# How many gate/up pairs of a feed-forward are multiplied directly before the seven-product form takes over

## The chip, the cores and the metric

The kernel runs on one core of a Trainium2 chip. The metric is the device time of one execution in microseconds (us). PE is TensorE, which multiplies matrices; DVE is VectorE, ACT is ScalarE, POOL is GpSimd, and SP is SyncE, which issues most of the transfers.

## The reference

The program computes a four-stage, two-layer streaming encoder on 512 tokens of 1024 features, in float32. Each layer is

```
x += 0.5 * SwiGLU_1(norm(x))
x += Mixer(norm(x))            # layer 0: two attentions; layer 1: gated conv and band attention
x += CrossAttn(norm(x), norm(mem))
x += 0.5 * SwiGLU_2(norm(x))
```

and a SwiGLU (a feed-forward) is

```
g, u = split_cols(h @ w_in, (D_FF, D_FF))      # w_in: 1024 x 5632, D_FF = 2816
return (silu(g) * u) @ w_out                   # w_out: 2816 x 1024
```

There are four feed-forwards: layer 0 first and second, layer 1 first and second. They are called FF1 to FF4 here, in the order in which they run.

## The kernel before, in words

**Precision.** Every float32 operand is split into a high and a low part of type float32r, and a product is three matmuls (`mm3`, high by high, high by low, low by high). ACT makes the high part, DVE the low part (a subtraction). This holds for the weights too: each weight chunk arrives in a tile `raw`, is split into two tiles `w`, and PE reads those. Six `w` tiles and three `raw` tiles circulate.

**A feed-forward in blocks.** The 2816 hidden columns are 22 blocks of 128. A gate/up pair is one block of the gate and the same block of the up projection. The blocks are worked in three parts (`PARTS`: 7, 7 and 8 pairs); behind each part comes its share of the output projection (`out_proj`, tiles `ps_o`), which adds into `x`.

**Two ways to multiply a pair.** The direct way (`proj_t`) needs 8 steps of 3 matmuls for the gate and as many for the up projection, 48 matmuls with 512 columns each. It reads `xh` and `xl`, the split of x times the gain, and the norm's factor (`rrow`) is multiplied in afterwards by DVE (`gate`, `up`: tiles `gs`, `us`). The block way (`Pair`) treats gate and up, the two halves of the 1024 features and the two halves of the tokens as a 2x2 block product and needs seven products instead of eight: 7 products of 4 steps of 3 matmuls with 256 columns, 84 matmuls. It needs sums of weight blocks, which `Sums` makes with an accumulating transfer from POOL's queue and two additions on POOL (tiles `s`), and sums of the normalized activations.

**The block operands.** `Norm.seven` makes these activation sums once per feed-forward: in four rounds (kk = 0 to 3) DVE makes seven half-token tiles (`hn`), ACT writes their high parts and DVE their low parts (tiles `bop`). It can start when `rrow` is there. It needs one slot for `hn` and seven for `bop`, out of nine slots (`tok_slot`); the `hn` slot is given back at its end.

**What runs first.** The first `FILL = 3` pairs of a feed-forward are multiplied the direct way, the other 19 in blocks. In FF1 alone the first pair's gate and up are multiplied together, feature by feature as x arrives (`pair_t`).

**What sets the order.** The order of all engines' instructions is written out ahead of time by a planner (`Sched`): each task is a generator that says what it needs, `price` charges every instruction to a clock of its engine, and at each step the task of the best priority whose needs are met by PE's planned clock goes next. Weight splits have priority 2, `seven` 3, the constants' set-up (`setup`) 4, the main line of matmuls 5; the gate and up tasks and the evacuations have 0 or 1. A price is nothing but a number for the order; on the chip each engine runs its list in that order and waits for semaphores.

**Where a pair's result goes.** The product silu(gate) times up is split and kept until the output projection. In the first part the pairs up to the last direct one but one lie in slots (tiles `gated`, two pairs to a slot); the last direct pair and those behind it reuse the memory of `xh`/`xl` (tiles `gh`, `gl`), which is free when the last direct matmul has read it.

Of the kernel before, what the change touches and what calls it, by code (L numbers as in the profile page):

```python
# [22 lines left out]
S = 512  # L23
# [5 lines left out]

FILL = 3  # L30
HS = S // 2
# [94 lines left out]
class Sched:  # L126
# [39 lines left out]
    def price(self, eng, method, outs, ins):  # L166
# [6 lines left out]
        if eng == "pe":  # L173
            if method == "transpose":
                cost = 0.108
            elif ins[0].dtype == F32R:
                cost = (n + 32) / 2400.0 if n >= 256 else 0.213
            else:
                cost = 0.06
# [88 lines left out]
def tile_trunk(ctx: ExitStack, tc: tile.TileContext, a: dict, out: bass.AP, nsteps: int = 8):  # L268
# [521 lines left out]

    def ffn_plan(w_in, w_oa, w_ob):
        for pi, (j0, j1) in enumerate(PARTS):
            last = None
            for j in range(j0, j1):
                if j < FILL:
                    plan_t(w_in[j])
                    plan_t(w_in[NF + j])
                    continue
# [12 lines left out]
    class Pair:  # L811
# [101 lines left out]
        def end(self):  # L913
# [14 lines left out]
            yield Need([g])  # L928
            gh, gl = self.res()
            yield from split(gh, gl, g)  # L930
            tok_gs.give()
            self.res.ev.set()

    class Gated:


        def __init__(self, tiles, j, where):
            self.tiles, self.j, self.where = tiles, j, where
            self.ev = Event()
            tiles[j] = (None, None, self.ev)  # L940

        def __call__(self):
            if isinstance(self.where, int):
                hi, lo = (cp.tile([P, S], F32R, tag=f"x{c}{self.where}", name=f"g{c}{self.where}")
                          for c in "hl")
            else:
                hi, lo = self.where[:, 0, :], self.where[:, 1, :]
            self.tiles[self.j] = (hi, lo, self.ev)
            return hi, lo

    def ffn(nrm, done):
# [12 lines left out]
        def up(pair, ps, res):  # L964
# [11 lines left out]
            yield Need([gs])  # L976
            gh, gl = res()
            yield from split(gh, gl, gs)
            tok_gs.give()
            res.ev.set()  # L980

        sch.add(nrm.seven(), 3)
        for pi, (j0, j1) in enumerate(PARTS):
            gated, ns, last = {}, 0, None
            for j in range(j0, j1):


                if pi == 0 and j >= FILL - 1:
                    where = j - FILL + 1
                elif pi == 1:  # L990
# [3 lines left out]
                else:  # L994
                    i = j - j0 - 4 * (pi == 2)
                    if i % 2 == 0:
                        yield tok_slot
                        ns += 1
                        sl = slot([2, 2, S], "gated")
                    where = sl[:, i % 2]  # L1000
                res = Gated(gated, j, where)
                if j < FILL:
                    r, pair = [], [Event()]
# [878 lines left out]
    for kind, layer in steps:  # L1882
# [7 lines left out]
        else:  # L1890
            ffn_plan(a[f"{kind}_in{layer}"], a[f"{kind}_oa{layer}"], a[f"{kind}_ob{layer}"])

# [129 lines left out]
```

## Time and profile before

| | us |
|---|---|
| median of three runs | 2306.8 (2306.78 to 2311.2) |
| the profiled execution | 2306.97 |
| its span, first to last instruction | 2305.2 |
| PE busy | 2224.7 (97%) |
| DVE busy | 1462.9 (63%) |
| ACT busy | 1086.7 (47%) |
| POOL busy | 569.1 (25%) |
| granted TensorE clock, mean | 0.987 |

The page of the profile has the busy time of each engine, the span in 40 slices, the transfer queues, the chain of work that ended last, the costliest groups of instructions with the idle time ahead of them, and the transfers. A group is a line, engine, operation and tile names; since all operations go through one helper, almost every row says L106, and the tile names tell the rows apart. Matmuls are pipelined, so that a matmul's own duration (some 290 to 390 ns) is longer than its share of a dense stream; a stream's length divided by its count gives the pace. FF1 runs from 6.7 to about 381 us of the span, FF2 from about 842, FF3 from about 1200 and FF4 from about 1948 us.

### The profile page before, as it was taken

To read this page: it belongs to the slowest core of one execution; us is meant where nothing else is said; L and a number is where in the kernel's file an instruction comes from. 1 tells how busy PE (TensorE), PEld (TensorE's weight loads), DVE (VectorE), ACT (ScalarE), POOL (GpSimd) and SP (SyncE) were. 2 spreads that over 40 slices of the span, in tenths; PEclk is the share of its full clock that TensorE was granted. 3 is DMA by queue.
4 is the path that set the end of the run, shared out by engine and by line. 5 is a ranking of instruction groups with operands and counts; after the bars stand their busy time and mean duration, and the time that the engine had idled before them with its cause. 6 is when DMAs were issued, how large, how long until landed. Compare 5 with 4: busy or idle time off the path is not lost.

```text
span 2305.2 us, 35767 instructions
## 1 busy us (share of the span) xinstructions
PE 2224.7 (97%) x14060; PEld 1993.9 (86%) x14060; DVE 1462.9 (63%) x2327; ACT 1086.7 (47%) x1869; POOL 569.1 (25%) x516
## 2 busy tenths in 40 slices
PE   7899999899999998999998999999999999899999
PEld 5889998889878888899987898989888888789897
DVE  8656575466666677465757564755675667847473
ACT  5535354455554444353544353545543554435352
POOL 2432322432311022222322131414112101213140
PEclk9899999999999999999999999999999999999999
DMA  5465652112232343555544464623123233346472
GB/s 174 113 185 144 176 148 87 65 56 85 90 101 82 101 119 96 151 148 154 163 123 110 126 171 136 182 98 115 53 81 127 93 110 107 111 131 165 136 187 83
DMA packets 108889, 281.56 MB, mean 122 GB/s; under 512 B 11896, under 2 KB 13944, under 8 KB 108720
## 3 DMA queue, kind: packets, MB, share of 16 engines
q1 hardware_dynamic: 84608, 233.94, 30.9%
q0 software_dynamic: 24112, 45.34, 11.0%
q8 instruction: 110, 1.80, 0.3%
q14 instruction: 59, 0.48, 0.1%
HBM read 277.11 MB, written 4.21 MB: 122 GB/s over the span
## 4 chain that ended last, share of the span: by engine, by line
PE 77%; DVE 9%; issue 4%; POOL 4%; DMA 3%; ACT 3%; SPq 0%; POOLq 0%; ACTq 0%; DVEq 0%
PE ps_m L106 46%; PE ps_o L106 24%; DMA s<-ffn_in 2%; DVE w L106 2%; DVE bop L106 2%; POOL qrr L106 1%; PE ps_pv L106 1%; DVE hn L106 1%; POOL qe L106 1%; ACT w L106 1%; PE ps_s L106 1%; DVE xl L106 1%; PE ps_x L106 1%; PE xo L106 1%; PE ps_pt L106 1%
## 5 line engine op out<-in xcount | busy, mean ns | idle before, releaser
L106 PE MATMUL ps_m<-bop,w 128*128 128x256 f32 x6384 | 787.0, 286 | 48.1 <-ACT bop L106 27.5
L106 PEld LDWEIGHTS ps_m<-bop,w 128*128 128x128 f32 x6384 | 781.7, 194 | 54.8 <-ACT bop L106 28.6
L106 ACT ACTIVATE w<-raw 128x1024 fp32r<-128x1024 f32 (+2 forms) x327 | 335.0, 1028 | 426.5 <-PE ps_o L106 240.2
L106 DVE TENSOR_TENSOR w<-raw,w 128x1024 fp32r<-128x1024 f32 (+2 forms) x327 | 396.1, 1211 | 153.9 <-ACT w L106 145.3
L106 POOL TENSOR_TENSOR s<-s,raw 128x512 f32<-128x512 f32 x152 | 231.2, 1521 | 438.8 <-DMA s<-ffn_in 270.0
L106 PE MATMUL ps_o<-gh,w 128*128 128x512 f32 x1024 | 328.1, 389 | 0.0
L106 PE MATMUL ps_m<-xh,w 128*128 128x512 f32 (+1 forms) x848 | 278.4, 396 | 1.2 <-ACT w L106 1.2
L106 DVE TENSOR_TENSOR w<-s,w 128x512 fp32r<-128x512 f32 (+1 forms) x228 | 219.1, 961 | 71.4 <-ACT w L106 47.4
L106 ACT ACTIVATE w<-s 128x512 fp32r<-128x512 f32 (+1 forms) x228 | 174.2, 768 | 121.6 <-POOL s L106 41.7
L106 PEld LDWEIGHTS ps_o<-gh,w 128*128 128x128 f32 x1024 | 192.3, 188 | 39.5
L106 DVE SCALAR_TENSOR_TENSOR x<-ps_o,x 128x512 f32<-128x512 f32 x160 | 108.5, 687 | 182.4 <-PE ps_o L106 182.0
L106 PE MATMUL ps_m<-w,xh 128*128 128x256 f32 x1152 | 218.9, 289 | 0.0
L106 PE MATMUL ps_o<-gl,w 128*128 128x512 f32 x512 | 199.4, 389 | 0.0
L106 PEld LDWEIGHTS ps_m<-xh,w 128*128 128x128 f32 (+1 forms) x848 | 158.1, 187 | 37.6 <-ACT w L106 2.1
L106 POOL DMA_DIRECT2D s<-ffn_in x76 | 92.0, 1210 | 373.8 <-DMA s<-ffn_in 285.2
L106 PEld LDWEIGHTS ps_m<-w,xh 128*128 128x128 f32 x1152 | 179.2, 191 | 2.0 <-issue 1.2
L106 PE MATMUL ps_m<-xl,w 128*128 128x512 f32 (+1 forms) x424 | 166.0, 392 | 0.0
L106 PE MATMUL ps_m<-w,xl 128*128 128x256 f32 x576 | 162.7, 282 | 0.0
L106 PE MATMUL ps_o<-gated,w 128*128 128x512 f32 x576 | 141.2, 389 | 0.0
L106 POOL TENSOR_TENSOR acc<-acc,sq 128x512 f32<-128x512 f32 x42 | 68.7, 1637 | 254.3 <-ACT sq L106 253.4
L106 PEld LDWEIGHTS ps_o<-gated,w 128*128 128x128 f32 x576 | 107.6, 188 | 22.0
L106 PEld LDWEIGHTS ps_o<-gl,w 128*128 128x128 f32 x512 | 96.2, 188 | 19.4
(468 smaller groups left out, 2826.9 us busy)
## 6 DMA issues: line engine op xcount, KB each, us to landing
raw<-ffn_in SPq DMA_DIRECT2D x98, 512.0 KB, 4.8
s<-ffn_in SPq DMA_DIRECT2D x76, 512.0 KB, 4.3
s<-ffn_in POOLq DMA_DIRECT2D x76, 512.0 KB, 5.9
raw<-ffn_oa SPq DMA_DIRECT2D x64, 448.0 KB, 3.4
a<-ffn_in SPq DMA_DIRECT2D x76, 256.0 KB, 3.8
raw<-ffn_ob SPq DMA_DIRECT2D x32, 512.0 KB, 3.5
raw<-x_kv SPq DMA_DIRECT2D x32, 512.0 KB, 3.5
raw<-even_w SPq DMA_DIRECT2D x24, 512.0 KB, 3.4
```

What stands on the lines that cost most here:

```text
L106: r = fn(*args, **kw)
```

## The change

The number of direct pairs becomes five in FF1 and four in the others. The planner's price of a float32r matmul loses its constant: columns over 2400, not columns plus 32. And since five or four direct pairs leave three or four results for slots, which are two slots beside the eight of `seven`, the slot of a result is now taken when the result is split (`Gated.take` waits for it, `Half` shares it between two pairs), and no longer by the main line ahead of the products.

```
-FILL = 3
+FILL = {True: 5, False: 4}
...
-                cost = (n + 32) / 2400.0 if n >= 256 else 0.213
+                cost = n / 2400.0 if n >= 256 else 0.213
...
-    def ffn_plan(w_in, w_oa, w_ob):
+    def ffn_plan(w_in, w_oa, w_ob, fill):
...
-                if j < FILL:
+                if j < fill:
...
-            gh, gl = self.res()
+            gh, gl = yield from self.res.take()
...
+    class Half:
+        def __init__(self):
+            self.ev = Event()
...
-        def __call__(self):
+        def take(self):
...
-                hi, lo = self.where[:, 0, :], self.where[:, 1, :]
+                if self.first:
+                    yield tok_slot
+                    self.where.slot = slot([2, 2, S], "gated")
+                    self.where.ev.set()
+                yield self.where.ev
+                i = 1 - self.first
+                hi, lo = self.where.slot[:, 0, i, :], self.where.slot[:, 1, i, :]
...
-            gh, gl = res()
+            gh, gl = yield from res.take()
...
+        fill = FILL[nrm.first]
...
-                if pi == 0 and j >= FILL - 1:
-                    where = j - FILL + 1
+                if pi == 0 and j >= fill - 1:
+                    where = j - fill + 1
...
-                    if i % 2 == 0:
-                        yield tok_slot
+                    first = i % 2 == 0
+                    if first:
                         ns += 1
-                        sl = slot([2, 2, S], "gated")
-                    where = sl[:, i % 2]
-                res = Gated(gated, j, where)
-                if j < FILL:
+                        half = Half()
+                    where = half
+                res = Gated(gated, j, where, first)
+                if j < fill:
...
+                     FILL[(kind, layer) == steps[0]])
```

Three places of the written-out order show what moves. The first is DVE's list in FF2, around the last round of the block operands (`hn`, then `bop`). Before:

```order
L106 SCALAR_TENSOR_TENSOR hn<-hn 128x256 x2
L106 TENSOR_TENSOR gated<-gs,gated 128x512
L106 TENSOR_TENSOR w<-s_8729,w 128x1024
L106 TENSOR_TENSOR us<-ps_m,rrow 128x512
L106 TENSOR_TENSOR gs<-gs,us 128x512
L106 TENSOR_TENSOR bop<-hn,bop 128x3x256
L106 TENSOR_TENSOR bop<-hn,bop 128x4x256
L106 TENSOR_TENSOR gl_9028<-gs,gh_9027 128x512
L106 TENSOR_TENSOR g<-ps_m,u 128x256
```

With the change:

```order
L107 SCALAR_TENSOR_TENSOR hn<-hn 128x256 x2
L107 TENSOR_TENSOR gated<-gs,gated 128x512
L107 TENSOR_TENSOR w<-raw,w 128x1024
L107 TENSOR_TENSOR us<-ps_m,rrow 128x512
L107 TENSOR_TENSOR gs<-gs,us 128x512
L107 TENSOR_TENSOR w<-raw,w 128x1024
L107 TENSOR_TENSOR bop<-hn,bop 128x3x256
L107 TENSOR_TENSOR bop<-hn,bop 128x4x256
L107 TENSOR_TENSOR gated<-gs,gated 128x512
L107 TENSOR_TENSOR gs<-ps_m,rrow 128x512
L107 TENSOR_TENSOR w<-s_8824,w 128x512
L107 TENSOR_TENSOR us<-ps_m,rrow 128x512
```

The split of a weight sum (`w<-s`) that stood ahead of the last `bop` rows has gone behind them, with another one that stood further up; in their place stand the split of the fourth pair's up weights and that of the first block pair's first chunk (both `w<-raw`). The third pair's `gated` split and the fourth pair's gate stand behind the last `bop` rows.

The second is ACT's list in FF1, where the constants are set up. Before, this stands between two evacuations (`u`) of the second block pair of the first part:

```order
L106 ACTIVATE v__629<-ps_m 128x256
L106 ACTIVATE e_gcol<-e_gcol 128x1
L106 ACTIVATE o_gcol<-o_gcol 128x1
L106 ACTIVATE e_gcol<-e_gcol 128x1
L106 ACTIVATE setup<-setup 128x64
L106 ACTIVATE subln<-subln 128x1
L106 ACT_TABLE_LOAD
L106 ACTIVATE lsm<-lsm 128x2
```

With the change it stands in the second part, behind that part's first products:

```order
L107 ACTIVATE w<-s_1022 128x1024
L107 ACTIVATE w<-raw 128x1024
L107 ACTIVATE e_gcol<-e_gcol 128x1
L107 ACTIVATE o_gcol<-o_gcol 128x1
L107 ACTIVATE e_gcol<-e_gcol 128x1
L107 ACTIVATE setup<-setup 128x64
L107 ACTIVATE subln<-subln 128x1
L107 ACT_TABLE_LOAD
```

The same work has moved whole from the first part of FF1 into its second part.

The third is PE's list in the mixer of layer 0, around its first transposes of a query tile (`qt`), which wait for POOL's scaling of `qe`. Before:

```order
L106 MATMUL ps_m<-w,xl_3719 128x256
L106 MATMUL ps_m<-w,xh_3626 128x256 x2
L106 MATMUL ps_m<-w,xl_3627 128x256
L106 MATMUL ps_m<-w,xh_3637 128x256 x2
L106 MATMUL ps_m<-w,xl_3638 128x256
L106 MATMUL qt<-ident,qe 128x128 x4
L106 MATMUL ps_m<-w,xh_3679 128x256 x2
```

With the change:

```order
L107 MATMUL ps_m<-w,xh_3597 128x256 x2
L107 MATMUL ps_m<-w,xl_3598 128x256
L107 MATMUL ps_m<-w,xh_3505 128x256 x2
L107 MATMUL ps_m<-w,xl_3506 128x256
L107 MATMUL qt<-ident,qe 128x128 x4
L107 MATMUL ps_m<-w,xh_3516 128x256 x2
```

The buffers have other numbers. Counted from the mixer's first projection matmul, 126 of them stood ahead of these transposes before, and 135 stand there now; of the next three groups of `qt` transposes the counts go from 156, 222 and 252 to 168, 225 and 258.

More of the change, by code (lines that the diff above doesn't have):

```diff
@@ L932, in end, with __init__ @@
             self.res.ev.set()
+    class Half:
+        def __init__(self):
+            self.ev = Event()
     class Gated:
-        def __init__(self, tiles, j, where):
-            self.tiles, self.j, self.where = tiles, j, where
+        def __init__(self, tiles, j, where, first=False):
+            self.tiles, self.j, self.where, self.first = tiles, j, where, first
             self.ev = Event()
             tiles[j] = (None, None, self.ev)
-        def __call__(self):
+        def take(self):
             if isinstance(self.where, int):
@@ L985, in ffn @@
             for j in range(j0, j1):
-                if pi == 0 and j >= FILL - 1:
-                    where = j - FILL + 1
+                first = False
+                if pi == 0 and j >= fill - 1:
+                    where = j - fill + 1
                 elif pi == 1:
@@ L1890, in tile_trunk @@
         else:
-            ffn_plan(a[f"{kind}_in{layer}"], a[f"{kind}_oa{layer}"], a[f"{kind}_ob{layer}"])
+            ffn_plan(a[f"{kind}_in{layer}"], a[f"{kind}_oa{layer}"], a[f"{kind}_ob{layer}"],
+                     FILL[(kind, layer) == steps[0]])
     def store(d):
```

## The prediction, made before the changed kernel was run

> **What bounds the kernel now.** I read the page's engine table first, then the costliest groups with their idle time, then PE by stretches, then PE's timeline where it is idle. The engine table and two groups:
>
> ```profile
> span 2305.2 us, 35767 instructions
> PE 2224.7 (97%) x14060; PEld 1993.9 (86%) x14060; DVE 1462.9 (63%) x2327; ACT 1086.7 (47%) x1869; POOL 569.1 (25%) x516
> ...
> L106 PE MATMUL ps_m<-bop,w 128*128 128x256 f32 x6384 | 787.0, 286 | 48.1 <-ACT bop L106 27.5
> ...
> L106 PE MATMUL ps_o<-gh,w 128*128 128x512 f32 x1024 | 328.1, 389 | 0.0
> ```
>
> PE is busy 97% of the span and idle 80.5 us. Of that idle time 48.1 us stand ahead of the block matmuls, and most of it waits for `bop`, the block operands that DVE and ACT make at the start of each feed-forward. PE by stretches (columns: stretch, length, busy time of PE, PEld, DVE, ACT, POOL, then granted clock, DMA share, GB/s) shows where:
>
> ```profile
> 43.00:86.00 43.00, 25.40 (x159) 23.89 (x158) 31.70 (x62) 20.38 (x38) 18.23 (x37) 0.72 0.36 103
> 381.00:640.00 259.00, 246.21 (x1858) 218.40 (x1856) 160.70 (x323) 140.49 (x294) 92.06 (x110) 1.00 0.23 75
> 640.00:682.00 42.00, 37.90 (x187) 30.25 (x186) 27.66 (x56) 23.38 (x51) 2.07 (x6) 0.96 0.31 101
> 871.30:905.00 33.70, 24.33 (x181) 23.80 (x181) 24.96 (x35) 15.63 (x25) 8.71 (x6) 0.85 0.46 130
> 905.00:1193.00 288.00, 288.00 (x1939) 267.60 (x1939) 171.40 (x244) 129.35 (x206) 71.33 (x51) 1.00 0.51 142
> 1552.00:1720.00 168.00, 163.54 (x1107) 143.77 (x1106) 105.58 (x222) 83.43 (x168) 44.50 (x54) 1.00 0.26 83
> ```
>
> Away from its start a feed-forward has no gap at all (288.00 of 288.00): there only the number and pace of the matmuls count. At its start PE stands still and the granted clock falls to 0.72 and 0.85. The two mixers leave 12.8 + 4.1 us and 4.5 us idle.
>
> **The pace of the two forms.** Two unbroken pieces of the chain of waits (start, length, what) give it:
>
> ```profile
> 1070.75 77.75 PE ps_m L106 x648
> 1034.68 36.07 PE ps_o L106 x159
> ```
>
> A block matmul of 256 columns takes 77.75 / 648 = 0.120 us, one of 512 columns 36.07 / 159 = 0.227 us. So a block pair is 84 x 0.120 = 10.08 us of PE and a direct pair 48 x 0.227 = 10.89 us: each swap costs 0.81 us, and the change makes five (two in FF1, one in each other), 4.0 us. The old price (columns plus 32) met this pace; the new one is below it.
>
> The Trainium skill, "TensorE: Matmul & The Clock Gate", section "Back-to-back issue gap", has columns/2.4 plus 2.5 ns, which is 109 and 216 ns; by that rule a swap would be an estimated 10.36 - 9.17 = 1.19 us and the five 5.9 us. It speaks against the change more than the trace does; the two rows above differ from it, and they decide.
>
> **The stall that the swaps cover, FF2 to FF4.** PE's timeline around FF2's first block products, and where the output projection begins in FF2, FF3 and FF4 with the first block matmul of FF3 and FF4 (a bracket is the idle time before and its releaser):
>
> ```profile
> 871.34 1.23 PE L106 MATMUL ps_m<-bop,w 128*128 128x256 f32 x9
> 878.55 0.58 PE L106 MATMUL ps_m<-bop,w 128*128 128x256 f32 x1 [5.98 <-ACT bop L106]
> 882.52 38.55 PE L106 MATMUL ps_m<-bop,w 128*128 128x256 f32 x302 [3.39 <-DVE bop L106]
> ...
> 921.07 2.06 PE ps_o L106 x9
> ...
> 1229.24 1.23 PE L106 MATMUL ps_m<-bop,w 128*128 128x256 f32 x9
> ...
> 1279.36 2.07 PE ps_o L106 x9
> ...
> 1977.34 1.23 PE L106 MATMUL ps_m<-bop,w 128*128 128x256 f32 x9
> ...
> 2027.03 2.07 PE ps_o L106 x9
> ```
>
> From the first block matmul to the output projection pass 49.73, 50.12 and 49.69 us, 149.5 together. In each lie four block pairs less the 24 matmuls that stand behind the projection's first nine: 312 x 0.120 = 37.4 us. So each loses some 12.3 us, of which 5.98 + 3.39 = 9.4 are idle and the rest slower matmuls at the lowered clock. The same skill page, section "What's actually happening", halves the clock after an idle window of about 3.4 us; the low clock behind the 5.98 us wait agrees. If the waits that remain are shorter, the clock should hold.
>
> With the change, 48 direct and 228 block matmuls stand there: 10.89 + 27.36 = 38.25 us, 114.8 for the three. That is 34.8 us less, minus what waits remain. For those I walk along DVE in FF2, which is the engine that is late:
>
> ```profile
> 846.30 0.69 DVE L106 TENSOR_TENSOR gs<-ps_m,rrow 128x512 f32<-128x512 f32 x1 [0.35 <-ACT rrow L106]
> ...
> 862.36 2.15 DVE L106 TENSOR_TENSOR bop<-hn,bop 128x256 fp32r<-128x256 f32 x3
> ...
> 868.86 1.22 DVE L106 TENSOR_TENSOR w<-raw,w 128x1024 fp32r<-128x1024 f32 x1
> 870.00 0.68 DVE L106 TENSOR_TENSOR gs<-ps_m,rrow 128x512 f32<-128x512 f32 x1
> 870.60 0.68 DVE L106 TENSOR_TENSOR w<-s,w 128x512 fp32r<-128x512 f32 x1
> 871.20 4.30 DVE L106 TENSOR_TENSOR bop<-hn,bop 128x512 fp32r<-128x512 f32 x3
> ...
> 877.66 0.88 DVE L106 SCALAR_TENSOR_TENSOR hn<-hn 128x256 f32<-128x256 f32 x2
> ...
> 881.52 2.08 DVE L106 TENSOR_TENSOR bop<-hn,bop 128x768 fp32r<-128x768 f32 x2
> ...
> 871.43 3.79 POOL L106 TENSOR_TENSOR s<-s,raw 128x512 f32<-128x512 f32 x2 [11.83 <-DVE w L106]
> ```
>
> DVE works nearly without a gap from 846.3 to 883.6. In the changed list the same stretch, up to the last `bop`, has one 1024-column split more (1.22), one 512-column split less (0.68) and the same eleven gate and up steps: the operands are ready at about 884.1. Where POOL adds at the same time a `bop` round takes 4.30 instead of 2.15 us; the additions stand later in the changed program, since their loads come behind the fourth pair's, but may still hit the last rounds, so I leave that cost in. PE now comes there at 871.34 + 10.89 = 882.2, and needs the last round nine matmuls later, at 883.3: 0.8 us of wait in place of 9.4.
>
> Two things are late next. The fourth pair's up weights are split only behind the third round's batch and the fourth `hn` batch, at 878.5 (the end of the `hn` row above) less 0.7 for the sum's split that has gone, plus 0.6 for a `gated` split and 1.1 of its own, so 879.5 with POOL's additions in the way (two rounds, 2.15 each) and 875.2 without; PE wants them half a pair after 871.34, at 876.8: between 0 and 2.7 us. And behind the last `bop` DVE's list has a `gated` split, a gate, two steps of the up projection and two weight splits (0.6 each, the last 1.2 us, some 5 together), while the third product wants the last of them 36 matmuls (4.3 us) after the first: about 1 us. What waits on DVE's queue behind these is only the next pair's evacuation, which has a bank of its own. I take 3 us per feed-forward (bounds 0.5 and 6): 34.8 - 9 = **25.8 us** saved (17 to 33).
>
> **FF1.** Its first block matmuls and the start of its output projection:
>
> ```profile
> 43.02 0.63 PE L106 MATMUL ps_m<-bop,w 128*128 128x256 f32 x4
> ...
> 50.49 0.58 PE L106 MATMUL ps_m<-bop,w 128*128 128x256 f32 x1 [6.17 <-ACT bop L106]
> ...
> 76.08 28.95 PE L106 MATMUL ps_m<-bop,w 128*128 128x256 f32 x216 [3.23 <-ACT u L106]
> 104.87 1.55 PE L106 MATMUL ps_o<-gated,w 128*128 128x512 f32 x6
> ...
> 59.39 2.18 DVE L106 TENSOR_TENSOR bop<-hn,bop 128x768 fp32r<-128x768 f32 x2
> ```
>
> Here 61.85 us pass for the same 37.4 us of matmuls. With two pairs more ahead it is 96 x 0.227 + 144 x 0.120 = 39.1 us, 22.8 less, minus what remains. The operands came at 61.6 in the old program (last row); two more direct pairs put the block products at 43.0 + 21.8 = 64.8, and DVE's list up to the last `bop` has three 1024-column splits of chunks and two gate steps more (3.7 + 1.3) and the splits of one sum of 512 and one of 1024 columns less (0.7 + 1.2), about 3 us more: again just in time. What does not vanish is the set-up of the constants, the 3.23 us wait for `u` behind it on ACT. It moves from a stretch that was stalled anyway into the second part, where PE had no other wait; I charge it in full, with a little lower clock, 4 us, and 2 us for late weights and the first evacuation. That is 6 (bounds 2 and 12), so **16.8 us** saved (11 to 21).
>
> **The price.** A cheaper matmul makes the planner put more matmuls between a task and what it waits for. In the steady feed-forward this changes nothing, PE has no gap there. In the mixers it does; the PE waits of layer 0's mixer and its end (waited for: total, times, longest):
>
> ```profile
> PE qt L106 <- POOL qe L106: 8.6, 11, 1.4
> PE kt_ps L106 <- DVE ke L106: 1.8, 1, 1.8
> PE ps_pt L106 <- DVE P L106: 1.6, 5, 0.4
> ```
>
> The transposes wait 0.8 us on average; the first four groups now stand 9, 12, 3 and 6 matmuls later, 0.4 to 1.4 us. But some of the later ones stand earlier, and a task put back can hold up the next. Of the 21.4 us idle in both mixers I expect **6 us** back; at best some 12, and at worst 4 lost, about half of the `qt` wait again.
>
> **The transfers.** Five pairs fewer need five accumulating transfers and ten POOL additions fewer; they end no chain in the steady part, so I count nothing. The ninth slot: only `seven` and two `gated` slots compete, and the list puts the third pair's split behind the last `bop`, so nothing on PE's path waits for it.
>
> **Sum.** 25.8 + 16.8 + 6 = 48.6 us from the profiled execution's 2306.97 (its span plus 1.8 us around it), which stands at the median of the runs shown, 2306.8: **2258 us**, 2.1% less. With all bounds at their good end 66 us go (2241), at their bad end 24 (2283).
>
> **Rivals.**
>
> 1. *DVE stays the bound.* Each direct pair brings DVE two 1.22 us splits and four 0.65 us steps, 5 us; if all of it lands ahead of the operands, `seven` ends 5 us later in FF2 to FF4 and 10 later in FF1, and 6 to 7 of the 12.3 us stay: three times 34.8/3 - 6.5 = 5.1, FF1 22.8 - 11, together 27 us: 2280. For it, DVE has no slack from 846.3 to 883.6; against it, the changed list carries only 0.5 us more there. Chance 0.12.
> 2. *The looser order hurts the mixers.* Transposes and what hangs on them stand later by a few matmuls each; if the end of the mixers is put off as much as they idle now (17 us in layer 0), 2307 - 42.6 + 17 = 2281. For it, the new price misses the measured pace by 6 to 11%; against it, the waits it lengthens are on engines with 47 and 63% of work. Chance 0.07.
> 3. *Slower: the slots.* If the `gated` results took their two slots before `seven` has its eighth, the last `bop` round would wait for a slot and the stall would stand behind the added pairs as long as it was. Then the swaps cost 4.0 us and nothing is won: 2311. It decides as soon as one `gated` tile precedes the last `bop` rows in the third or fourth pair's place. Against it, the list has the rows the other way round. Chance 0.03.
> 4. *The change does little*, since the planner gives the direct pairs no more lead than before: 2305 to 2309. Chance 0.02.
>
> **How the numbers follow.** My forecast has 0.76. The range 2240 to 2282 takes in its bounds and the first two rivals. A difference of 0.2% (4.6 us) is what a measurement of this kernel can tell from none. Faster: 0.76 + 0.12 + 0.07 = 0.95; same 0.02; slower 0.03.
>
> **What would show it.** Right: the idle time ahead of `ps_m<-bop` falls from 48.1 to about 10 to 15 us, with 5964 such matmuls instead of 6384; the granted clock stays at or near 1.00 at the starts of FF2 to FF4; from the first direct matmul of the fourth pair to the output projection of FF2 pass about 41 us; the `qt` waits shrink. Wrong: a wait of over 4 us for `bop` in FF2 to FF4 (rival 1), more PE idle time than 17 us in layer 0's mixer (rival 2), or a DVE wait for a slot in the `bop` rows (rival 3).

## The result, and the profile after

The changed kernel takes 2250.7 us (median of 4 runs, 2247.8 to 2253.2), the kernel before on the same chip 2306.8: a ratio of 0.9753, 95% interval 0.9736 to 0.9771. The forecast was 2258 in a range of 2240 to 2282. The profiled execution took 2253.2, with a span of 2251.3. Its page has, of the rows shown of before:

```profile
span 2251.3 us, 35196 instructions
PE 2213.8 (98%) x13880; PEld 1979.2 (88%) x13880; DVE 1446.7 (64%) x2302; ACT 1073.0 (48%) x1839; POOL 553.3 (25%) x501
...
L107 PE MATMUL ps_m<-bop,w 128*128 128x256 f32 x5964 | 728.0, 284 | 17.7 <-DVE g L107 9.2
```

The idle time ahead of the block matmuls has fallen from 48.1 to 17.7 us, and what ends it is no longer `bop` but `g`, DVE's evacuation of a product. To see where the time came from, the profiled execution is cut at points that PE's timeline shows in every kernel: the first matmul of the norm's broadcast (`rb`), and in each output projection the first matmul behind the part's last block product, which is some 5 us behind the projection's very first one (888.95 and 884.01 us in FF2 with the change). "FF1 first part" runs from the start of the span to the cut in its first output projection; "mixer 0" from the cut in FF1's last output projection to FF2's broadcast (with the rest of that projection and the cross attention in it); "FF2" from there to its first cut; "mixer 1" likewise before FF4.

| us | FF1 first part | FF1 second | FF1 third | mixer 0 | FF2 | FF3 | mixer 1 | FF4 |
|---|---|---|---|---|---|---|---|---|
| before | 111.3 | 110.0 | 120.7 | 503.1 | 80.8 | 81.2 | 438.7 | 80.8 |
| after | 90.2 | 121.0 | 119.4 | 485.5 | 72.8 | 75.2 | 434.4 | 73.5 |
| difference | -21.1 | +11.0 | -1.3 | -17.6 | -8.0 | -6.0 | -4.3 | -7.3 |

The eight make -54.6; all other stages together +0.7; the two spans differ by 53.9. By the prediction's three terms that is 21.3 us in FF2 to FF4 (forecast 25.8), 11.4 in FF1 (16.8) and 21.9 in the mixers (6). The first two came short by 9.9, the third was 15.9 over.

**FF2 to FF4.** PE's timeline from the first block matmul to the output projection, of FF2, FF3 and FF4 (brackets: idle time before, and what ended it):

```profile
853.37 4.80 PE L107 MATMUL ps_m<-bop,w 128*128 128x256 f32 x38
859.18 14.41 PE L107 MATMUL ps_m<-bop,w 128*128 128x256 f32 x118 [1.01 <-DVE w L107]
874.87 9.31 PE L107 MATMUL ps_m<-bop,w 128*128 128x256 f32 x72 [1.28 <-DVE g L107]
884.01 2.23 PE L107 MATMUL ps_o<-gated,w 128*128 128x512 f32 x9
...
1203.45 4.81 PE L107 MATMUL ps_m<-bop,w 128*128 128x256 f32 x38
...
1226.07 10.64 PE L107 MATMUL ps_m<-bop,w 128*128 128x256 f32 x72 [2.40 <-DVE g L107]
1236.55 2.23 PE L107 MATMUL ps_o<-gated,w 128*128 128x512 f32 x9
...
1941.83 3.03 PE L107 MATMUL ps_m<-bop,w 128*128 128x256 f32 x24
...
1964.04 1.69 PE L107 MATMUL ps_m<-bop,w 128*128 128x256 f32 x12 [1.58 <-DVE g L107]
...
1973.18 2.00 PE L107 MATMUL ps_o<-gated,w 128*128 128x512 f32 x8
```

No wait for `bop` is left. From the first row of each group to its last pass 30.64, 33.10 and 31.35 us, where the 228 matmuls between them would take 27.36: 3.3, 5.7 and 4.0 us of losses remain. The chain behind FF2's 1.28 us wait, on POOL, ACT and DVE:

```profile
863.56 1.21 POOL L107 DMA_DIRECT2D s<-ffn_in  x1 [5.51 <-DVE w L107]
871.28 2.65 POOL L107 TENSOR_TENSOR s<-s,raw 128x512 f32<-128x512 f32 x2 [6.50 <-DMA s<-ffn_in]
...
872.60 0.63 ACT L107 ACTIVATE w<-s 128x512 fp32r<-128x512 f32 x1 [3.82 <-POOL s L107]
873.13 0.61 ACT L107 ACTIVATE g<-g 128x512 f32<-128x512 f32 x1
...
873.26 1.22 DVE L107 TENSOR_TENSOR w<-s,w 128x512 fp32r<-128x512 f32 x1 [3.52 <-ACT w L107]
874.40 0.41 DVE L107 SCALAR_TENSOR_TENSOR g<-ps_m,g 128x256 f32<-128x256 f32 x1
```

A weight sum's accumulating transfer is issued at 863.56 and its addition starts at 871.28, when it has landed; then ACT splits the sum, then DVE. DVE stands still for 3.52 us for that split, and in its list the evacuation `g` stands behind it. PE waits for `g`. What `g` needs of ACT (`g<-g`) stood behind the same split in ACT's list, but was there at 873.74, 0.7 us before DVE came to `g`; what held it at the end was its place in DVE's list.

**FF1's second part.** PE, ACT, DVE and POOL in their timelines:

```profile
144.75 16.14 PE L107 MATMUL ps_m<-bop,w 128*128 128x256 f32 x120 [2.44 <-ACT u L107]
...
171.24 1.70 PE L107 MATMUL ps_m<-bop,w 128*128 128x256 f32 x12 [1.18 <-DVE g L107]
...
184.94 1.69 PE L107 MATMUL ps_m<-bop,w 128*128 128x256 f32 x12 [2.79 <-DVE g L107]
...
195.24 0.44 PE L107 MATMUL ss<-ident,setup 128*128 128x128 f32 x2 [1.73 <-POOL setup L107]
...
138.19 1.28 ACT L107 ACT_TABLE_LOAD   x1
...
140.21 1.28 ACT L107 ACT_TABLE_LOAD   x1
...
144.34 0.36 ACT L107 ACTIVATE u<-ps_m 128x256 f32<-128x256 f32 x1
...
183.49 0.42 ACT L107 ACTIVATE setup<-mem 128x256 f32<-128x256 f32 x1 [3.55 <-DMA mem<-mem]
...
184.46 0.42 DVE L107 SCALAR_TENSOR_TENSOR g<-ps_m,g 128x256 f32<-128x256 f32 x1 [3.26 <-ACT g L107]
...
125.79 0.63 POOL L107 DMA_DIRECT2D setup<-lam  x1
```

Nearly all of it is the set-up of the constants. Its first transfer is issued at 125.79 (before: 61.87), since `setup` takes a slot for its scratch, and the nine slots were held by seven `bop` tiles and two `gated` ones until the first output projection had read them. It then lands in a part where PE had one short wait before. ACT's `u` stands behind the constants and two loads of function tables (2.44 us of PE), the evacuation `g` waits for an ACT that waits 3.55 us for a block of `mem` (2.79 us of PE), and the row of 1.73 waits for mem's sum itself. The row of 1.18 ends in the split of a weight sum, whose addition comes late on POOL (167.64) among the steps of mem's sum. The four rows make 8.1 us.

**The mixers.** Windows over mixer 0 (length, busy PE, PEld, DVE, ACT, POOL, clock, DMA share, GB/s), of before:

```profile
342.00:845.00 503.00, 483.88 (x2995) 414.92 (x2995) 314.68 (x590) 258.96 (x506) 125.12 (x139) 1.00 0.26 84
```

and of after, the whole and the tail that answers to the 42 us at clock 0.96 shown of before:

```profile
330.60:816.00 485.40, 478.22 (x2997) 413.62 (x2996) 317.02 (x590) 257.92 (x506) 127.81 (x139) 1.00 0.27 87
624.00:666.00 42.00, 42.00 (x206) 34.94 (x205) 32.56 (x57) 27.84 (x53) 8.34 (x10) 1.00 0.35 113
```

Idle time fell from 19.1 to 7.2 us, and PE's busy time for the same matmuls by 5.7. Of that, 1.7 us are the lowered clock of before: taken by stretches of 10 us it is 1.00 in all but one, where it is 0.83, and in the changed kernel in all. The rest comes at least in part from fewer breaks: where a stream stops, its last matmul counts with its full 0.28 us and not with its share of 0.12, and before there were 25 waits, now 10; 15 x 0.16 is an estimated 2.4. The waits that remain:

```profile
PE qt L107 <- POOL qe L107: 4.3, 6, 1.1
PE ss L107 <- DVE acc L107: 2.2, 3, 1.1
PE ps_pt L107 <- DVE P L107: 0.2, 1, 0.2
```

Half of the `qt` wait has gone, and the waits for `ke`, `xkv`, `pl`, `k` and `xot` wholly.

### The profile page after: what moved, and what is told of

It reads as the page before. It is cut to its first block, busy times and chain, and to the rows that moved or that the text cites. A ratio compares the mean times of both kernels' runs of the same rounds, so it can differ in the third digit from the quotient of the medians.

```text
span 2251.3 us, 35196 instructions
## 1 busy us (share of the span) xinstructions
PE 2213.8 (98%) x13880; PEld 1979.2 (88%) x13880; DVE 1446.7 (64%) x2302; ACT 1073.0 (48%) x1839; POOL 553.3 (25%) x501
## 4 chain that ended last, share of the span: by engine, by line
PE 79%; DVE 10%; issue 3%; POOL 3%; DMA 3%; ACT 2%; SPq 0%; POOLq 0%; DVEq 0%; ACTq 0%
PE ps_m L107 44%; PE ps_o L107 27%; DVE w L107 3%; DMA s<-ffn_in 2%; DVE hn L107 2%; PE ps_pv L107 2%; DVE bop L107 2%; PE ps_s L107 1%; PE ps_x L107 1%; PE xo L107 1%; PE ps_pt L107 1%; DVE xl L107 1%; POOL s L107 1%; ACT w L107 1%; POOL qe L107 1%
## 5 line engine op out<-in xcount | busy, mean ns | idle before, releaser
L107 PE MATMUL ps_m<-bop,w 128*128 128x256 f32 x5964 | 728.0, 284 | 17.7 <-DVE g L107 9.2
L107 PEld LDWEIGHTS ps_m<-bop,w 128*128 128x128 f32 x5964 | 722.9, 193 | 23.9 <-DVE g L107 10.2
L107 PE MATMUL ps_m<-xh,w 128*128 128x512 f32 (+1 forms) x1008 | 328.8, 396 | 2.1 <-ACT w L107 2.1
L107 POOL TENSOR_TENSOR s<-s,raw 128x512 f32<-128x512 f32 x142 | 214.5, 1510 | 405.4 <-DMA s<-ffn_in 221.8
L107 PE MATMUL ps_o<-gh,w 128*128 128x512 f32 x944 | 302.5, 389 | 0.0
L107 PEld LDWEIGHTS ps_m<-xh,w 128*128 128x128 f32 (+1 forms) x1008 | 188.2, 187 | 44.9 <-ACT w L107 2.7
L107 PE MATMUL ps_m<-xl,w 128*128 128x512 f32 (+1 forms) x504 | 197.2, 391 | 0.0
L107 PE MATMUL ps_o<-gated,w 128*128 128x512 f32 x696 | 168.6, 389 | 0.0
L107 PEld LDWEIGHTS ps_o<-gated,w 128*128 128x128 f32 x696 | 130.1, 188 | 26.6
L107 POOL TENSOR_TENSOR acc<-acc,sq 128x512 f32<-128x512 f32 x42 | 73.7, 1755 | 246.7 <-ACT sq L107 245.6
L107 PEld LDWEIGHTS ps_m<-xl,w 128*128 128x128 f32 (+1 forms) x504 | 94.5, 187 | 18.7
```

The costliest lines, as they stand in the source:

```text
L107: r = fn(*args, **kw)
```

## The experiments

The stages of all kernels, cut as above, with medians and ratios to the kernel before on the same chip (before: 2306.7 for the first four, 2307.5 for the next four, 2307.4 for the three after them, 2310.0 for the last). A stage comes from one profiled execution; the rest of the program, outside the eight stages above, varies between 778.6 and 783.6 us from kernel to kernel, so that a difference of a us or two in one stage is not firm:

| | FF1 1st | FF1 2nd | mixer 0 | FF2 | FF3 | mixer 1 | FF4 | median | ratio (95%) |
|---|---|---|---|---|---|---|---|---|---|
| old price | 91.4 | 131.2 | 501.7 | 73.1 | 74.3 | 439.0 | 73.0 | 2285.1 | 0.9909 (0.9892-0.9925) |
| price alone | 109.9 | 111.6 | 485.2 | 79.7 | 80.3 | 434.4 | 79.5 | 2284.5 | 0.9901 (0.9887-0.9916) |
| set-up in own scratch | 97.3 | 112.4 | 485.3 | 73.5 | 74.6 | 434.4 | 75.0 | 2255.4 | 0.9773 (0.9758-0.9787) |
| four in FF1 | 95.6 | 120.7 | 485.2 | 73.5 | 72.6 | 434.5 | 72.8 | 2255.7 | 0.9775 (0.9761-0.9790) |
| five everywhere | 88.2 | 118.4 | 485.6 | 70.6 | 70.5 | 434.4 | 70.3 | 2244.9 | 0.9728 (0.9713-0.9742) |
| lower price | 87.6 | 116.5 | 500.2 | 72.5 | 74.7 | 434.8 | 72.8 | 2266.3 | 0.9826 (0.9809-0.9843) |
| set-up at the projection | 89.0 | 137.0 | 485.6 | 73.7 | 72.4 | 434.4 | 72.9 | 2267.6 | 0.9830 (0.9815-0.9844) |
| old price, more lag | 89.2 | 130.2 | 513.1 | 71.6 | 71.5 | 439.4 | 71.6 | 2289.0 | 0.9920 (0.9903-0.9936) |
| mem's sum off POOL | 89.0 | 117.0 | 485.1 | 73.0 | 73.2 | 434.3 | 73.8 | 2249.0 | 0.974 (0.972-0.976) |
| five, mem's sum off POOL | 89.0 | 118.8 | 485.1 | 70.3 | 70.3 | 434.5 | 70.3 | 2239.3 | 0.9698 (0.9674-0.9721) |
| the same, own scratch | 98.3 | 110.1 | 485.3 | 70.7 | 71.0 | 434.4 | 70.3 | 2242.4 | 0.9712 (0.9691-0.9733) |
| the same, at the projection | 91.0 | 129.6 | 485.3 | 70.6 | 70.8 | 434.4 | 70.3 | 2251.6 | 0.9745 (0.9728-0.9761) |

### The pairs alone, and the price alone

The changed kernel with the old price. With it the plan would come to a point where the third pair's result holds the slot that `seven` needs for its last tile, so that result is made to wait for the operands; by the planner's lists this extra line changes no engine's order at the new price, which no run shows.

```
-                cost = n / 2400.0 if n >= 256 else 0.213
+                cost = (n + 32) / 2400.0 if n >= 256 else 0.213
...
+                    if self.after is not None:
+                        yield self.after
...
+                res.after = nrm.bev[3] if pi == 0 and j == 2 else None
```

> The changed kernel with the old price of a matmul (columns plus 32). The third pair's result here waits for the last block operands before it takes its slot; in the changed kernel that leaves every engine's list as it was, and with the old price it keeps the planner from giving that slot away too early. Theory: the stretch from FF1's last output projection to FF2's norm (mixer and cross of layer 0) got 17.6 us shorter and the like stretch of layer 1 4.3 us because of the price alone, so this run loses about 20 us again: 2268 to 2274 us, with the starts of FF2 to FF4 as short as in the changed kernel (within 3 us each). Rival: those stretches got shorter because the feed-forwards now hand over other buffers and transfers: then 2249 to 2255 us.

The new price with three pairs everywhere:

```
-FILL = {True: 5, False: 4}
+FILL = {True: 3, False: 3}
```

> The changed kernel with three direct pairs in every feed-forward; the new price stays. Theory: the price is worth about 22 us in the mixers whatever the feed-forwards do, and the waits for the block operands come back (about 48 us idle ahead of those matmuls): 2281 to 2289 us. The set-up of the constants finds a slot early again and the second part of FF1 takes about 110 us, not 121. Rival: the price does little by itself: 2300 to 2308 us.

Measured: 2285.1 and 2284.5 us. The second is as expected, with 45.5 us of idle time ahead of the block matmuls; the first misses its 2268 to 2274, though the mixers lose the 20 us that were expected (16.2 and 4.6). The price alone takes 17.9 us from mixer 0 and 4.3 from mixer 1, whatever the number of pairs; the pairs alone take 1.4 there and give 0.3 back. So the mixers' 21.9 us belong to the price. The starts of FF2 to FF4 belong to the pairs: 7.7, 6.9 and 7.8 us with the old price, about 1 each with the new price alone. Neither alone is worth more than 22.2 us, both together 56.1: the old price makes FF1's second part 131.2 instead of 121.0, and that is most of what the two lack to the sum, and most of what the first run missed. Both runs take a result's slot late, as the changed kernel does; that part of the change was not tried alone.

### The set-up in scratch of its own

The set-up's scratch comes out of two tiles that lie free in FF1, so that it need not wait for a slot.

```
-        yield tok_slot
-        st = slot([8, 256], "setup", F32)
+        yield tok_q
+        yield tok_q
+        st, st2 = (tp.tile([P, 2, 256], F32, tag="qe", name="setup") for _ in range(2))
...
```

> The changed kernel, with the set-up's scratch in two tiles of another pool instead of a slot, so that it need not wait until the first output projection gives a slot back. Theory: the second part of FF1 took 121 us instead of 110 because the set-up came only then and stands between the weight sums on POOL; with its own memory it starts some 60 us earlier, that part falls to 110 to 113 us, and the first part gets the 3 to 5 us wait behind the set-up on ACT: 2241 to 2247 us. Rival: that part is slow because two block pairs instead of four in the first part leave less time for its loads: then it stays at 119 to 122 us and the time at 2249 to 2254.

Measured: the second part falls to 112.4, as it should if the slot is what makes the set-up late. But the first part takes 97.3 instead of 90.2, and the total (2255.4) misses what was expected. PE and ACT in its first part:

```profile
75.97 15.90 PE L107 MATMUL ps_m<-bop,w 128*128 128x256 f32 x120 [8.76 <-ACT u L107]
...
68.00 1.28 ACT L107 ACT_TABLE_LOAD   x1
71.14 0.20 ACT L107 ACTIVATE lsm<-lsm 128x2 f32<-128x2 f32 x1 [1.85 <-DVE lsm L107]
71.36 1.28 ACT L107 ACT_TABLE_LOAD   x1
...
75.56 0.37 ACT L107 ACTIVATE u<-ps_m 128x256 f32<-128x256 f32 x1
```

From 67.4 to 75.6 us ACT does nothing but the constants: two table loads, and between them waits for the small steps of DVE. The evacuation `u` stands behind, and PE waits 8.76 us. In the changed kernel the same block costs 2.44. There ACT needs 6.8 us for it instead of 8.2 (137.56 to 144.34), since DVE's first steps come 1.3 us sooner behind it, and PE still had 4.7 us of products in hand when it began (its stream ends at 142.3), where here it runs dry about when the block begins.

### Four pairs in FF1

```
-FILL = {True: 5, False: 4}
+FILL = {True: 4, False: 4}
```

> Four direct pairs in FF1 too, not five. Theory: the block operands of FF1 are ready at about 63 us and the fourth pair ends at about 55: PE waits some 7 to 9 us there and the clock falls, less 0.8 us for the swap saved: 2256 to 2261 us. Rival: FF1 is bound by its transfers and the fifth pair only delays them: 2247 to 2252 us.

Measured: 2255.7, just under the 2256 to 2261 that were expected, the first part 95.6. PE's waits in it are for the block operands again:

```profile
PE ps_m L107 <- DVE bop L107: 5.0, 1, 5.0
PE ps_m L107 <- ACT bop L107: 2.3, 1, 2.3
```

The fifth pair takes these away and costs 0.81 of its own; it is worth 5.4 us in the stage.

### Five pairs everywhere

```
-FILL = {True: 5, False: 4}
+FILL = {True: 5, False: 5}
```

> Five direct pairs in every feed-forward. Theory: with four pairs no matmul of FF2 to FF4 waits for the block operands any more, so a fifth only adds its 0.8 us each, and the later waits (for the weight sums' splits and the evacuations behind them) stay or move: 2250 to 2256 us, the first parts of FF2 to FF4 0 to 2 us longer than in the changed kernel. Rival: the waits that are left are still the start's, and a longer lead takes away another 2 us each: 2243 to 2247 us.

Measured: 2244.9, the rival's case. The starts take 70.6, 70.5 and 70.3 us: the fifth pair pays its 0.81 us and still saves 2.2, 4.7 and 3.2 us against four. The total alone doesn't show it, since its interval touches the changed kernel's; the stages do: all four kernels with five pairs have 70.3 to 71.0 us there, and all with four at the new price 72.4 to 75.2. PE's wait for `g` falls from 9.2 to 2.9 us in the whole program. The weight sums of the first block pairs are wanted a pair later. The prediction had treated the stall as covered once `bop` was there.

### A lower price, and the old price with more lag

If the mixers gain because the planner puts more between a task and what it waits for, a still lower price should gain more, and the old price with a longer assumed delay from engine to engine should gain too. The first has the columns less 32 as its price; both carry the extra line of the first experiment.

```
-                cost = n / 2400.0 if n >= 256 else 0.213
+                cost = (n - 32) / 2400.0 if n >= 256 else 0.213
```

> A price lower still: columns minus 32 over 2400. Theory: the mixers' PE waits that are left (6.9 us in layer 0, 2.3 in layer 1) shrink a little more, as transposes stand still later: the stretch to FF2 2 to 5 us shorter, the time 2244 to 2250 us. Rival: the price that was found is the best, and with a lower one the tasks put back hold up the next ones: 2252 to 2262 us.

```
-    LAG = {"pe": 0.2, "act": 0.15, "dve": 0.14, "pool": 0.08, "dma": 2.0, "swdge": 2.2}
+    LAG = {"pe": 0.5, "act": 0.45, "dve": 0.44, "pool": 0.38, "dma": 2.0, "swdge": 2.2}
...
-                cost = n / 2400.0 if n >= 256 else 0.213
+                cost = (n + 32) / 2400.0 if n >= 256 else 0.213
```

> The changed pairs with the old price, but with 0.3 us more of lag charged to PE's, ACT's, DVE's and POOL's results in the planner. Theory: the price helps the mixers by putting more matmuls between a task and its need; charging the others' results later does the same at the right price, so most of the 17.9 and 4.3 us come back: stretch to FF2 485 to 492 us, and a time of 2250 to 2268 us. Rival: the price helps by the order in which weight splits and evacuations follow each other, not by the lead: the stretch stays near 500 us and the time near 2285.

Measured: mixer 0 takes 500.2 and 513.1 us instead of 485.5. Both theories fall. Counted from FF1's last output projection matmul, the mixer's own output projection starts after 220.6 us before, 207.6 after, 191.9 at the lower price and 199.4 with more lag: up to there more lead does gain. What follows takes it back. The stretch from 600 to 660 us of the span, which lies in mixer 0 in all of them, in the changed kernel, at the lower price, and with more lag:

```profile
600.00:660.00 60.00, 60.00 (x317) 48.89 (x316) 43.56 (x86) 36.63 (x74) 8.82 (x16) 1.00 0.35 114
```

```profile
600.00:660.00 60.00, 55.56 (x268) 43.80 (x269) 37.51 (x80) 34.37 (x74) 14.30 (x24) 0.91 0.27 91
```

```profile
600.00:660.00 60.00, 51.18 (x261) 39.25 (x261) 34.43 (x81) 30.59 (x70) 16.70 (x25) 0.86 0.27 87
```

PE stands still there for steps of the attention on DVE and ACT (`Pa`, `mn`, `ph`, `pl`), with 268 and 261 matmuls in the stretch instead of 317, and the granted clock falls to 0.91 and 0.86. That too few projection matmuls are left to cover these steps is what the rows suggest; no run tests it. Of the 14.7 us that mixer 0 loses at the lower price 5.9 are idle time (13.1 instead of 7.2), and the rest is longer busy time, at a clock of 0.98 over the whole stage. So the gain isn't "the more lead the better"; of the prices tried, the new one gives the order that loses least. Which of the moved groups decides the tail is not settled by these runs.

### Where the set-up could go

Five kernels look for what makes the set-up dear. In the first it starts beside FF1's first output projection, in its own scratch:

```
+    def late_setup(nrm):
+        sch.add(setup(nrm.bev[3]), 4)
+        return
+        yield
...
+                                ((late_setup(nrm),) if pi == 0 and nrm.first else ()), read)
...
-        sch.add(setup(nrm.bev[3]), 4)
...
```

> The changed kernel with the set-up's scratch in two tiles of its own and its start put behind the last block products of FF1's first part, so that it runs beside that part's output projection. Theory: the set-up costs what it costs because it shares ACT, DVE and POOL with block pairs, 7 us in the first part (the run with its own memory) or 10 us in the second (the changed kernel); beside the output projection those engines are less than half busy: first part 90 to 91 us, second 110 to 114, time 2240 to 2245 us. Rival: the second part is slow for another reason: 119 to 122 us and 2249 to 2254.

Measured: 2267.6, the second part 137.0; the theory falls. PE and POOL around the longest wait, and the transfers of that stretch (KB each, median us from issue to landing):

```profile
170.23 4.99 PE L107 MATMUL ps_m<-bop,w 128*128 128x256 f32 x25 [13.71 <-DVE g L107]
...
143.68 2.23 POOL L107 DMA_DIRECT2D rel_d<-rel  x2
145.91 1.31 POOL L107 DMA_DIRECT2D s<-ffn_in  x1
166.69 2.61 POOL L107 TENSOR_TENSOR s<-s,raw 128x512 f32<-128x512 f32 x2 [19.47 <-issue]
...
rel_d<-rel POOLq DMA_DIRECT2D x2, 1024.0 KB, 17.8
```

I first put this down to POOL's in-order queue, with four steps of mem's sum ahead of a weight sum. The four kernels that follow test that: the eight loads of `mem` go to SyncE's queue and the seven additions to DVE.

```
-            swdge.dma_start(out=raw, in_=a["mem"][:, d, :])
+            sync.dma_start(out=raw, in_=a["mem"][:, d, :])
...
-                pool.tensor_tensor(acc, acc, sq, ALU.add)
+                dve.tensor_tensor(acc, acc, sq, ALU.add)
```

That edit in the changed kernel:

> The changed kernel, but the sum over mem's eight row blocks in the late set-up no longer touches POOL: its eight loads are issued by SyncE among the weight loads and its seven additions run on VectorE (0.4 us each). The set-up still waits for the same slot and starts at the same place. Theory (POOL's in-order queue is what makes the late set-up dear: a weight sum's accumulating transfer stands behind additions that wait for mem): the second part of the first feed-forward falls from 121.0 us to 111-115, the rest stays, total 2240-2246. Rival (the price comes from the set-up's other work, the tables of sines and the constants that enter DVE's and ACT's queues in the busiest stretch, or from the weight loads behind SyncE's extra eight): 118-124 us, total 2248-2255.

That edit with five pairs everywhere:

> The same move of mem's sum off POOL in the kernel with five pairs ahead in every feed-forward (2244.9 us, its second part 118.4). Theory: the two gains add, second part 110-114, total 2236-2241. Rival: second part 116-121, total 2243-2248.

That edit, five pairs, and the set-up in its own scratch:

> Five pairs ahead in every feed-forward, the set-up in scratch of its own (so it no longer waits for a slot and runs in the first part, as in the kernel whose first part took 97.3 us and second 112.4), and mem's sum off POOL. Theory (in the first part too it is POOL's queue that costs): the first part falls from 97.3 to 88-92, the second stays at 111-113, total 2229-2236. Rival (the first part is bound by VectorE, which the set-up loads wherever its sum runs): first part 96-101, total 2240-2248.

That edit, five pairs, and the set-up beside the first output projection:

> Five pairs ahead everywhere; the set-up in scratch of its own, started beside the first output projection of the first feed-forward (the place where the second part took 137.0 us), and mem's sum off POOL. Theory (there POOL's queue was the cause: the accumulating transfer of the second part's first weight sums stood behind four steps of mem's sum): the second part falls from 137.0 to 112-117 us, of which about 4 are the output projection's wait for ACT behind the constants, and the total is 2231-2238. Rival (the weights are late there because the constants and mem's loads delay the weight splits on ACT and SyncE's queue, whoever adds): second part 124-137, total 2246-2260.

Measured: 2249.0, 2239.3, 2242.4 and 2251.6 us. In the changed kernel the second part falls from 121.0 to 117.0, between the two expectations, and the total doesn't differ measurably (0.974 against 0.9753, intervals overlapping). PE's waits there are now 2.4 us for `u`, behind the constants as before, and 3.4 for mem's sum itself; those for `g` have gone. So in this profile mem's sum on POOL is worth about a third of the second part's 11.0 us. With five pairs the second part gets no shorter (118.8 against 118.4). There too the waits for `g` have gone, but behind the 3.0 us wait for mem's sum the clock is at 0.50 from 188.56 to 195.38 us, which costs an estimated 3.4 us; behind the like wait of 3.4 us, with that edit in the changed kernel, it stays at 1.00. The total of 2239.3 is inside the theory's range, but its interval overlaps that of five pairs alone (2244.9), so the edit's own worth isn't shown. In its own scratch the theory falls: the first part still takes 98.3, with one wait of 8.69 us for `u` behind the same block of ACT. Beside the projection it falls too: 129.6, with one wait of 9.82 us for `g`, though mem's sum has left POOL.

What the two kernels with the set-up beside the projection have in common is what the rows above show: the set-up ends with two transfers of 1024 KB (`rel_d`), issued on POOL, and the next weight sum's accumulating transfer is issued behind them. At the projection they are issued at 143.68 and 134.85, in the stretch where the second part's first weight sums are loaded, and the next sum's addition starts 20.8 and 13.6 us after its transfer was issued, against a median of 6.0 from issue to landing. POOL's queue is not all of it: in the last kernel SyncE's loads of `s`, `raw` and `a` between 125 and 165 us land after 9.1, 11.2 and 9.4 us, against 4.3, 4.9 and 4.0 in its whole program, and the sum's transfer itself is issued only at 147.62, since it waited 10.5 us for such a load. In the changed kernel the two are issued at 197.50, where the third part's sums are not yet wanted, and cost nothing to be seen. In the kernel with five pairs and its own scratch they are issued at 115.11; the sums' transfers behind them land after 17.6 us, and PE waits 0.5 us at most in that second part. So late sums cost only where they are soon wanted. A kernel with these two transfers alone put off wasn't tried, so that they are the cause rests on these rows, and whether the order of POOL's queue or the sharing of the transfer engines does it, they don't tell.

**The best version** is five pairs everywhere with mem's sum off POOL: 2239.3 us, 0.9698 of before (0.9674 to 0.9721), and faster than the changed kernel beyond both intervals. Its page:

```profile
span 2237.9 us, 34918 instructions
PE 2213.5 (99%) x13772; PEld 1976.1 (88%) x13772; DVE 1448.5 (65%) x2294; ACT 1066.5 (48%) x1821; POOL 528.7 (24%) x477
...
L107 PE MATMUL ps_m<-bop,w 128*128 128x256 f32 x5712 | 695.6, 284 | 4.7 <-ACT u L107 3.0
```

PE is busy for 99% of the span; 4.7 us of idle time are left ahead of the block matmuls.

## Why the prediction was right, and where it was wrong

- **Time and sign** came out: 2250.7 against 2258, inside the range. It owes some of that to errors of opposite sign: 9.9 us too much from the feed-forwards, 15.9 too little from the mixers.
- **The stall of FF2 to FF4, 25.8 us (17 to 33): right, a little high: 21.3 measured.** The operands were ready in time, as the walk along DVE's list had it: of the forecast 0.8 us wait for `bop` nothing is seen. The 1 us wait of the third product for the last weight split is there to the digit: 1.01 us at 38 matmuls. From the fourth direct pair (48 x 0.227 before the first block matmul at 853.37, so 842.5) to the output projection at 884.01 pass 41.5 us; 41 was forecast. 9 us of losses were charged and 13.0 are left (3.3, 5.7 and 4.0). What failed is "what waits on DVE's queue behind these is only the next pair's evacuation, which has a bank of its own". PE comes round to that evacuation all the same: at the 157th block matmul it waited 1.28, 2.40 and 1.58 us for `g`, which in FF2 stood behind the split of a late weight sum, as the chain above shows. Five pairs show it from the other side, with 2 to 5 us more saved per feed-forward.
- **FF1, 16.8 us (11 to 21): 11.4, at the low end.** The first part came out about as charged: 22.8 less 2 us of waits is 20.8, and measured are 19.6 to the projection's very first matmul (104.87 and 85.31) and 21.1 at the table's cut. The mis-sized term is the set-up, 4 us charged and 11.0 measured in the second part. The step that failed is the ninth slot: "only `seven` and two `gated` slots compete". The set-up competes too, and with scratch of its own the second part falls to 112.4. I had seen that its block moves into the second part, and priced the one row of before (3.23 us for `u`); that block cost 2.44. What I left out is everything of the set-up that comes behind it, mem's sum above all, which before ran before the second part's products, and now ran among them.
- **The price, 6 us (-4 to 12): 21.9, outside its bounds.** The sign and the place were right; the size is the term that was wrong. I bounded it by half of the waits shown, at most 12 of 21.4 us idle. But idle time in mixer 0 alone fell by 12 of 19, and 5.7 us more of busy time went with it, which a sum made from idle time alone cannot hold. The row with the clock at 0.96 in the 42 us tail stood in the prediction, and was not priced. Also, `ke`, `xkv`, `pl` and `k`, which I didn't count, are waits of the same kind, and all of them vanished. Nor is "more matmuls between a task and what it waits for" the whole mechanism: with still more of it the mixer loses again.
- **Rivals.** DVE as the bound: no wait for `bop` was left; fallen. The looser order hurting the mixers: fallen for this price, but the mechanism is real: with the old price and more lag mixer 0 takes 513.1 us, 10 more than before. The slots making `seven` wait: it didn't happen in the changed kernel; with the old price the planner would have met that very conflict, which no run shows, and the slots did hold up the set-up.
- **What would show it.** The idle time ahead of `ps_m<-bop` is 17.7 us (10 to 15 forecast), with the 5964 matmuls; the clock holds at 1.00 over the starts of FF2 and FF4, not over FF3's; the `qt` waits shrink.
- **The clock's rule**, by which the Trainium skill ("TensorE: Matmul & The Clock Gate", "What's actually happening") halves the clock after an idle window of about 3.4 us: with the waits gone it stays up in FF2 and FF4, as forecast. In FF3 it does not, behind a wait of 2.40 us, and the trace disagrees with that length (below).

## What to carry to other kernels

When a stall is covered, walk on past it: ask of every in-order queue what else stands ahead of the next thing that PE wants, and of every pool of buffers who else takes from it. A planner's price that is "wrong" can make a better order than a right one, because it changes which work is left as cover for later; the gain holds for one value and not for the direction, so try neighbours of it rather than reason from lead. Housekeeping that is moved into a stretch without slack costs through the evacuations queued behind it: here 11.0 us, where 4 had been charged.

## What the runs showed of the hardware that was not expected

**A pause of 2.4 us can halve the clock, and one of 2.8 can leave it alone: it depends on where the pause falls.** In the changed kernel the clock is at 0.50 from 145.56 to 148.98 us and from 1227.59 to 1231.00, each time for 3.41 us, and the two starts lie 317 times 3.413 us apart. So the clock seems to be set on a grid of 3.41 us. Cut on that grid, the stretches around the waits of 2.44 us (it ends at 144.75), 2.79 us (184.94) and 2.40 us (FF3, 1226.07) are these (busy PE first, the clock third from the end):

```profile
142.15:145.56 3.41, 0.97 (x8) 0.81 (x7) 2.15 (x11) 2.03 (x7) 1.37 (x6) 1.00 0.18 66
145.56:148.98 3.42, 3.42 (x18) 3.42 (x17) 1.85 (x4) 2.52 (x4) 3.32 (x4) 0.50 0.37 115
...
179.70:183.11 3.41, 2.45 (x21) 2.24 (x19) 1.23 (x1) 0.24 (x1) 0.95 (x1) 1.00 1.02 380
183.11:186.52 3.41, 1.58 (x12) 1.48 (x12) 1.30 (x3) 2.15 (x5) 2.48 (x3) 1.00 0.43 160
186.52:189.94 3.42, 3.26 (x27) 3.16 (x27) 3.34 (x6) 2.69 (x5) 1.53 (x2) 1.00 0.87 119
...
1224.18:1227.59 3.41, 1.52 (x12) 1.50 (x12) 2.35 (x4) 1.94 (x5) 0.95 (x1) 1.00 0.38 124
1227.59:1231.00 3.41, 3.31 (x16) 3.08 (x15) 2.76 (x6) 2.34 (x5) 0.00 (x0) 0.50 0.05 15
```

The 2.44 us wait lies whole in one stretch, where PE is busy for 0.97 us, and the next stretch has the clock at 0.50. Most of FF3's wait lies in one stretch, with 1.52 us busy, and the same follows, 1.5 us after PE is back. The 2.79 us wait is cut in two, with 2.45 and 1.58 us busy, and the clock stays. Behind FF3's wait 72 matmuls took 10.64 us, where the like 72 of FF2 took 9.31. The limit isn't sharp: with the set-up in its own scratch 1.49 us busy (112.96 to 116.37) are followed by 1.00, and with the old price and more lag 1.67 us (666.60 to 670.01) by 0.50.

The Trainium skill ("TensorE: Matmul & The Clock Gate", "What's actually happening") has free-running windows of 3.4 us, which fits the grid, and an idle window as the condition. None of these three waits leaves a whole window idle, and two were followed by the low clock, so the measured pauses speak against that condition as it stands.

**Big transfers on POOL's queue hold up the small ones behind them, and SyncE's too.** Two of 1024 KB (a median of 17.8 and 19.5 us to landing in the two kernels) stood ahead of a weight sum's transfer, whose addition came 20.8 and 13.6 us after its issue; at other times such a transfer lands in 6.0. SyncE's loads meanwhile took twice as long (9.1 to 11.2 us, against 4.0 to 4.9).
